# Gate and up of two SwiGLU FFNs: eight block products against seven

## The chip, the cores and the metric

One core of one Trainium2 chip runs the whole kernel. The metric is the device time of one execution in microseconds; a profile of one execution gives each engine's instructions within its span, from the first to the last instruction. TensorE is called PE here, VectorE DVE, ScalarE ACT, GpSimd POOL and SyncE SP; SP issues the DMAs.

## The reference

The kernel computes a two-layer decoder trunk on 512 tokens of 1024 features in float32. Each layer has a token mixer (sparse attention in layer 0, latent attention with an indexer in layer 1), a cross-attention to 256 memory rows, an output projection with a residual, and then a SwiGLU FFN with a residual; a last RMSNorm follows. What matters here is the FFN of each layer, in short:

```python
D_FF = -(-8 * D_MODEL // (3 * 256)) * 256          # 2816
xn = rmsnorm(x, norm_ffn[i])                       # [512, 1024]
h = silu(xn @ ffn_gate[i]) * (xn @ ffn_up[i])      # [512, 2816]
x = x + h @ ffn_down[i]                            # [512, 1024]
```

## The kernel before

**Arithmetic.** Every large product is made of three matmuls. An operand is split into a high part `hi` (the value rounded to the fp32r type) and a low part `lo` (the value minus `hi`); `mm3` (L266) adds hi x hi, hi x lo and lo x hi into one PSUM bank, on L267, L268 and L269. `split` (L213) makes the parts: ACT casts `hi` (L214), DVE subtracts to get `lo` (L215). `split_pool` (L225) does both on POOL, `split_ap` (L229) the cast on ACT and the difference on POOL.

**The FFN.** `ffn` (L592) cuts the 2816 hidden columns into 11 units of 256 and these into four parts, of 3, 3, 3 and 2 units. For a unit, `ffn_gu` (L587) loads 256 columns of gate and of up, 1 MB each, into two tiles `rawb` and splits each into two pieces of 128 columns x 8 k tiles (`whi`, `wlo`, 128x1024 each). For each 128 columns, gate and up are each one PSUM bank of 512 tokens, 8 k tiles x 3 matmuls of 512 columns. In the first unit of a layer the tokens are taken in two halves of 256 columns, so that it can begin when two token tiles have been normed. Then come Silu on ACT (L611), the product with up on DVE (L612) and a split of the result into a hidden tile pair `hh`, `hl`. After the units of a part the down product follows: for each half of the 1024 output columns four PSUM tiles, one for each token tile, over the part's k tiles, in groups of at most four k tiles; DVE adds the finished bank to the residual (L667, in the last part L646).

**Buffers.** `whi` and `wlo` have WBF = 4 buffers each in the FFN, `rawb` 2, the low hidden tiles `hl` 12. The high hidden tiles are held in pairs in the slots of the weight pool of the stage before (`hidden`, L118). PSUM has eight banks in four tags (L42): s 2, t 3, o 2, f 1; `phase` gives each role a string of tags that `bank` goes through in turn. In the FFN (PF, L49) role f, the gate and up banks, goes through o, o, f, t and role s, the down banks, through s, s, t. The tiles `fh`, `fl` (each 128 x 8 x 512) hold the split and transposed input X; `xh` and `xl` hold the concatenated heads until the output projection is done.

**Around it.** The last stage of `out_units` (L547) takes one token tile after another: output projection, residual, `norm_steps` (L174: squares on ACT, scale of the first 512 features on DVE, L207, of the second on POOL, L204 and L205), and `to_T` (L217: transposes on PE, L221, and a split into `fh`, `fl`). `before_ffn` (L982) opens the weight pool of the FFN and loads and splits the first unit ahead of it. In layer 0 `mem_kv1` (L1096), the keys and values of the memory for layer 1, runs after the gate and up of part 0 and before its down product (OTP = 0). In the last part of layer 0 the norm of layer 1 and its first projections (`in_proj`, L998) follow each token tile.

**What sets the order.** The tile framework orders each engine's instructions at compile time, by the order of the program and by when an operand and a buffer come free, so an engine may take a later step ahead of one that still waits. At run time each engine keeps to that order. SP takes the DMAs in its own fixed order; each waits for its slot.

Of the kernel before, what the change touches and what calls it, by code (L numbers as in the profile page):

```python
# [11 lines left out]
OP = mybir.AluOpType  # L12
# [36 lines left out]
PF = ("sst","","","ooft","ooft")  # L49
# [47 lines left out]
def tile_trunk(ctx: ExitStack, tc: tile.TileContext, A, out):  # L97
# [20 lines left out]
    def hidden():  # L118
        WP["n"] = WP.get("n", 0) + 1
        return WP["h"].tile([128, 2, 512], F32R, name=nm("hh"), tag=("raw", "whi", "wlo")[WP["n"] % 3], bufs=2)  # L120


# [10 lines left out]
    # ---------------------------------------------------------------- constants  # L133
# [10 lines left out]
    # ---------------------------------------------------------------- PSUM tiles: one bank each in the mixers  # L144
# [29 lines left out]
    def norm_steps(g, np_, use, by_pool, use_half=None):  # L174
        """(after the first half of the columns of a token tile, after the second half)"""
# [83 lines left out]
    def wsplit(src, by_col, where=None, eng=split):  # L259
        """src [128, a, b] in DRAM -> list of (hi, lo) pieces, cut along b (by 128) or along a"""  # L260
# [10 lines left out]
    def proj_T(xh, xl, nk, W, n, evac, N=512, tag="f", eng=split, where=None):  # L271
        """psum[cols 128, N] for each 128 columns of W [nk*128, n]"""
# [10 lines left out]
    def proj_tok(xh, xl, nk, load, n, evac, step, nt=NT, tag="f"):  # L283
        """psum[tokens 128, n] for each token tile, the weights [nk, 128, n] kept for all of them"""
# [14 lines left out]
    def stack_hl(p, scale, dsts):  # L299
        """p psum [128, N] of two heads -> per head [hi; lo] (even) and [lo; hi] (odd)"""  # L300
# [6 lines left out]
    def dup_hl(p, hi, lo):  # L307
        """p psum [64, ...] -> hi, lo on both halves of the partitions"""
# [4 lines left out]
    # ---------------------------------------------------------------- relative bias rows  # L313
# [34 lines left out]
    # ---------------------------------------------------------------- memory attention  # L348
    def mem_kv(i, xm, rs, wk, kv, slot, f32=False, where=None):
# [14 lines left out]
        proj_T(mt[:, 0], mt[:, 1], KD, W[:, 0:256], 256, ek, N=MEML, eng=ENG[MWK[i][0]], where=where)  # L364
# [9 lines left out]
        proj_tok(mt[:, 0], mt[:, 1], KD, rows(W[:, 256:512], where, ENG[MWK[i][1]]), 256, ev, 4, nt=2)  # L374
# [12 lines left out]
    def pt_piece(work, blocks, bufs, by_pool=False, wide=4):  # L387
        """transposes of [128, 128] blocks -> hi, lo [128, n*128]"""
# [22 lines left out]
    def pt_f32(work, blocks, bufs, wide):  # L411
        """transposes of [128, 128] blocks in float32"""
# [11 lines left out]
    def mem_attend(qm, kv, work, dst, f32=False):  # L424
        """a generator: one step for each pair of query tiles and pair of heads"""
# [161 lines left out]
    def ffn_gu(i, fp, c, eng=split):  # L587
# [4 lines left out]
    def ffn(i, fp, gu0, xh, xl, res, fin, early=None, other=None):  # L592
        Wd = A["ffn_down"][i]
        parts = [(0, 3), (3, 6), (6, 9), (9, 11)]
        for pi, (a, b) in enumerate(parts):
            hh, hl = [], []
            for c in range(a, b):
                gs, us = ffn_gu(i, fp, c) if c else gu0
                hp = hidden()
                for m in range(2):  # L600
                    pp = []
                    for wh, wl in (gs[m], us[m]):
                        p = bank("f")
                        first = c == 0
                        for n0, n1 in ((0, 256), (256, 512)) if first else ((0, 512),):
                            for k in range(KD):
                                mm3(p[:, n0:n1], wh[:, k], wl[:, k], xh[:, k, n0:n1], xl[:, k, n0:n1],
                                    k == 0, k == KD - 1)
                        pp.append(p)
                    sg = fp.tile([128, 512], F32, name=nm("sg"), tag="sg", bufs=2)  # L610
                    act.activation(sg, pp[0], AF.Silu)  # L611
# [721 lines left out]
```

## Time and profile before

| | |
|---|---|
| time of the runs | 1342.33, 1344.34, 1344.53 us (median 1344.34) |
| profiled execution, its span | 1342.6 us |
| PE, DVE, ACT, POOL busy | 1272.7, 724.5, 551.3, 285.6 us |
| matmuls | 6370 |
| mean granted clock | 0.985 of full speed |

The profile gives the profiled execution's span and no other time of its own; the span lies within the times of the runs, 1.7 us under their median. A row of a group reads: line, engine, operation, written tile <- read tiles, shape written <- shape read, count, then busy time in us and mean ns of one, and the idle time of the engine just before them with what ended it. Matmuls are pipelined and their ends are modelled, so that the busy time of several overlaps: their rate is read from their number in a stretch.

### The profile page before, as it was taken

Reading aid. Unit: us, or ns where it says so; the run is one execution under the profiler, and the core shown is the slowest. Engines: PE = TensorE matmul, PEld = TensorE weight load, DVE = VectorE, ACT = ScalarE, POOL = GpSimd, SP = SyncE. Lnnn points to the kernel's source line nnn. Section 1 sums busy time; section 2 is a strip of 40 time slices with the busy share of each in tenths; the row PEclk is TensorE's granted clock in tenths of the full one; section 3 lists DMA queues with packets and bytes.
Section 4 is the critical chain, followed back from the end, with each engine's and each line's share of the span. In section 5 each row is a group of like instructions: output and inputs, shape, how many; then the busy total and the mean of one; then the engine's idle time right before and its main releaser. Section 6 shows DMA issues by size and latency. Waiting matters only on the chain.

```text
span 1342.6 us, 17159 instructions
## 1 busy us (share of the span) xinstructions
PE 1272.7 (95%) x6370; PEld 1041.5 (78%) x6370; DVE 724.5 (54%) x1435; ACT 551.3 (41%) x1146; POOL 285.6 (21%) x442
## 2 busy tenths in 40 slices
PE   5989999999999999999999878999899999999997
PEld 5768889798878888888877655678788888888885
DVE  6475778987334333333445899769633333433325
ACT  6375557775322221221334465556432222222231
POOL 6440445635010000000005165552500000000001
PEclk9999999999999999999999989999899999999998
DMA  7742311223224322322321011324221321321311
GB/s 246 215 139 86 110 41 56 69 74 111 95 94 156 113 76 94 109 75 99 103 94 52 22 61 30 94 77 130 79 94 63 126 94 63 125 94 63 126 63 63
DMA packets 107703, 126.77 MB, mean 94 GB/s; under 512 B 5176, under 2 KB 82008, under 8 KB 107620
## 3 DMA queue, kind: packets, MB, share of 16 engines
q1 hardware_dynamic: 107620, 125.68, 28.8%
q8 instruction: 50, 0.82, 0.3%
q14 instruction: 33, 0.27, 0.1%
HBM read 122.22 MB, written 6.58 MB: 96 GB/s over the span
## 4 chain that ended last, share of the span: by engine, by line
PE 61%; DVE 5%; ACT 2%; POOL 2%; issue 1%; DMA 0%; POOLq 0%; DVEq 0%; ACTq 0%
PE f L267 13%; PE f L268 12%; PE f L269 12%; PE s L268 6%; PE s L269 6%; PE s L267 6%; PE o L532 1%; DVE sco L1131 1%; DVE m L1130 1%; PE t L416 1%; DVE sco L1060 1%; POOL xn L204 1%; PE o L464 0%; DVE sb L511 0%; POOL xn L205 0%
## 5 line engine op out<-in xcount | busy, mean ns | idle before, releaser
L214 ACT CAST whi<-rawb 128x1024 fp32r<-128x1024 f32 (+1 forms) x130 | 135.5, 1048 | 461.4 <-PE f L268 276.7
L267 PE MATMUL f<-fh,whi 128*128 128x512 f32 (+1 forms) x768 | 290.5, 380 | 1.9 <-ACT whi L214 1.2
L268 PE MATMUL f<-fl,whi 128*128 128x512 f32 (+1 forms) x768 | 290.6, 379 | 0.0
L269 PE MATMUL f<-fh,wlo 128*128 128x512 f32 (+1 forms) x768 | 290.2, 379 | 0.3 <-DVE wlo L215 0.3
L215 DVE TENSOR_TENSOR wlo<-rawb,whi 128x1024 fp32r<-128x1024 f32 (+1 forms) x130 | 161.1, 1241 | 220.9 <-ACT whi L214 216.9
L267 PEld LDWEIGHTS f<-fh,whi 128*128 128x128 f32 x768 | 145.8, 191 | 31.9 <-ACT whi L214 1.6
L269 PEld LDWEIGHTS f<-fh,wlo 128*128 128x128 f32 x768 | 145.8, 190 | 30.1 <-DVE wlo L215 0.7
L268 PEld LDWEIGHTS f<-fl,whi 128*128 128x128 f32 x768 | 145.8, 190 | 29.3
L183 POOL TENSOR_SCALAR ss<-ss 128x1 f32<-128x1 f32 x16 | 5.6, 350 | 689.2 <-ACT sq L181 689.2
L612 DVE TENSOR_TENSOR sg<-f,sg 128x512 f32<-128x512 f32 x44 | 30.4, 692 | 177.5 <-PE f L269 176.2
L268 PE MATMUL s<-wlo,hh 128*128 128x512 f32 x288 | 115.0, 399 | 0.0
L267 PE MATMUL s<-whi,hh 128*128 128x512 f32 x288 | 112.3, 394 | 0.0
L269 PE MATMUL s<-whi,hl 128*128 128x512 f32 x288 | 111.6, 390 | 0.0
L521 POOL TENSOR_SCALAR sb<-sb,sm 128x128 f32<-128x128 f32 (+3 forms) x144 | 76.6, 548 | 94.5 <-DVE sm L1218 44.7
L517 ACT ACTIVATE sb<-sb,mx 128x128 f32<-128x128 f32 (+3 forms) x144 | 79.5, 555 | 33.7 <-DVE mx L514 33.0
L511 DVE CUSTOM_DVE_ANT_0 sb<-s,M 128x512 f32<-128x512 f32 (+3 forms) x144 | 66.2, 483 | 13.8 <-PE t L416 4.6
L667 DVE TENSOR_TENSOR res<-s,res 128x512 f32<-128x512 f32 x48 | 32.9, 689 | 60.1 <-PE s L269 60.0
L267 PEld LDWEIGHTS s<-whi,hh 128*128 128x128 f32 x288 | 53.9, 187 | 14.2
L269 PEld LDWEIGHTS s<-whi,hl 128*128 128x128 f32 x288 | 54.1, 188 | 12.8
L268 PEld LDWEIGHTS s<-wlo,hh 128*128 128x128 f32 x288 | 54.0, 188 | 12.0
L215 DVE TENSOR_TENSOR ptl<-t,pth 128x512 fp32r<-128x512 f32 (+1 forms) x98 | 57.6, 603 | 4.7 <-ACT pth L214 3.7
L214 ACT CAST pth<-t 128x512 fp32r<-128x512 f32 (+1 forms) x98 | 48.8, 521 | 22.8 <-PE t L392 19.5
(363 smaller groups left out, 2495.4 us busy)
## 6 DMA issues: line engine op xcount, KB each, us to landing
rawb<-in_ffn_gate_dram SPq DMA_DIRECT2D x22, 1024.0 KB, 5.0
rawb<-in_ffn_up_dram SPq DMA_DIRECT2D x22, 1024.0 KB, 5.5
rawb<-in_ffn_down_dram SPq DMA_DIRECT2D x16, 1024.0 KB, 4.9
M<-relskew SPq DMA_DIRECT2D x36, 256.0 KB, 2.7
raw<-in_w_out_dram SPq DMA_DIRECT2D x16, 512.0 KB, 3.5
raw<-in_nsa_w_in_dram SPq DMA_DIRECT2D x12, 512.0 KB, 4.5
rawb<-in_ffn_down_dram SPq DMA_DIRECT2D x12, 512.0 KB, 3.4
relskew<-relrow SPq DMA_DIRECT2D x1, 3072.0 KB
```

The lines of the kernel that those rows point to most:

```text
L204: pool.tensor_scalar(dst[:, c], src[:, c], r, 0.0, op0=OP.mult, op1=OP.add)
L214: act.copy(hi, src)
L215: dve.tensor_sub(lo, src, f(hi))
L267: pe.matmul(o, ah, bh, start=start, stop=False)
L268: pe.matmul(o, ah, bl, start=False, stop=False)
L269: pe.matmul(o, al, bh, start=False, stop=stop)
L416: pe.transpose(p[:, j * 128:(j + 1) * 128], b, ident)
L511: dve.tensor_tensor_reduce(E[j, br].rearrange("p (k n) -> p k n", n=128), sv[:, :, x, :], Mi.rearrange("p (k n) -> p k n", n=128), 1.0, -3 ...
L517: act.activation(E[j, br], E[j, br], AF.Exp, bias=mx[:, j, br:br + 1], accum_out=sm[:, j, br:br + 1])
L521: pool.tensor_scalar(E[j, br], E[j, br], fc[:, j, br:br + 1], 0.0, op0=OP.mult, op1=OP.add)
L612: dve.tensor_mul(sg, pp[1], sg)
L667: dve.tensor_add(res[t][:, cs], acc[t], res[t][:, cs])
```

## The change

Gate and up are computed by a seven-product scheme on two-by-two blocks. A unit's gate and up weights are each cut into 2 x 2 blocks, A11, A12 (k tiles 0 to 3 and 4 to 7 of the first 128 columns) and A21, A22 (of the second); X is cut into four blocks by k half and token half (B11, B21 for tokens 0 to 255, B12, B22 for 256 to 511). Seven products of a block of weights (for gate and for up at once, 8 k tiles in all) with 256 tokens replace eight. On the X side the sums T1 to T4 are made once for a layer (`x_halves`), on the weight side four sums a unit, on POOL, in place in the raw tile (`gu_unit`). The partial sums are kept in two PSUM banks: four products add into `xb`, three into `z`, and what an output needs on the way is copied out (`c11`, `c12`, `c22`) or added (`tensor_add`).

With it go: a raw tile of 2 MB for a unit (`gu_load`; two buffers); PSUM roles X (tag o, two banks) and Z (tag f, one bank), transposes on tag t; hidden tiles of 128x1024 in eight slots (`hslot`), some of them lent from and to the norm's scratch (`Lent`); the first two products of the first two units taken ahead of the rest of the first unit, in place of the token halves; `mem_kv1` moved to the start of part 1, its memory rows now in a `rawb` slot and its transposes in hidden slots (`Two`); the last part's down weights in the piece slots (`wsplit`).

```diff
-PF = ("sst","","","ooft","ooft")
+PF = ("sst","","","t","t","o","f")
...
+    def hslot(dt=F32R):
+        tag = HS["order"][HS["n"] % len(HS["order"])]
+        HS["n"] += 1
+        where = HS["fp"] if tag == "hx" else WP["h"]
+        return where.tile([128, 1024], dt, name=nm("hh"), tag=tag, bufs=2)
...
-    def phase(s, t, o, f, x):
-        PS.update(s=s, t=t, o=o, f=f, x=x)
+    def phase(s, t, o, f, x, X="", Z=""):
+        PS.update(s=s, t=t, o=o, f=f, x=x, X=X, Z=Z)
...
+    def x_halves(fp):
+
+        fh, fl, th, tl = [big.tile([128, 2 if n == "fl" else 4, 4, 256], F32R, name=nm("X" + n), tag=n)
+                          for n in ("fh", "fl", "xh", "xl")]
+        X = dict(B11=fh[:, 0:2], B21=fh[:, 2:4], B22=fl[:, 0:2], T1=th[:, 0:2], T3=th[:, 2:4], T2=tl[:, 0:2],
+                 T4=tl[:, 2:4])
+        own = []
+
+        def use(t, xn):
+            if not own:
+                own.extend(WP["p"].tile([128, 4, 256], F32, name=nm("xf"), tag=x, bufs=WP["w"]) for x in ("whi", "wlo"))
+            f11, f21 = own
+            q = slice(t % 2 * 128, (t % 2 + 1) * 128)
+            for k0 in (0, 4):
+                p = bank("x")
+                for k in range(4):
+                    pe.transpose(p[:, k * 128:(k + 1) * 128], xn[:, (k0 + k) * 128:(k0 + k + 1) * 128], ident)
+                pv = p.rearrange("p (k q) -> p k q", k=4)
+                if t < 2:
+                    d = X["B21" if k0 else "B11"]
+                    split(pv, d[:, 0, :, q], d[:, 1, :, q])
+                    act.copy((f21 if k0 else f11)[:, :, q], pv)
+                elif k0 == 0:
+                    f12, t1, t3, t2, t4 = [ctile(fp, n).rearrange("p (k q) -> p k q", k=4)
+                                           for n in ("e", "c11", "c12", "c22", "c21")]
+                    dve.tensor_sub(t1, f11[:, :, q], pv)
+                    act.copy(f12, pv)
+                else:
+                    dve.scalar_tensor_tensor(t2, t1, -1.0, pv, op0=OP.mult, op1=OP.subtract)
+                    dve.tensor_sub(t3, pv, f12)
+                    d = X["B22"]
+                    split(pv, d[:, 0, :, q], d[:, 1, :, q])
+                    dve.scalar_tensor_tensor(t4, t2, -1.0, f21[:, :, q], op0=OP.mult, op1=OP.subtract)
+                    for n, x, eng in (("T2", t2, split), ("T1", t1, split_ap), ("T3", t3, split), ("T4", t4, split_ap)):
+                        eng(x, X[n][:, 0, :, q], X[n][:, 1, :, q])
...
+    def gu_load(i, fp, c):
         cs = slice(c * 256, (c + 1) * 256)
-        return [wsplit(A[n][i][:, cs].rearrange("(k p) c -> p k c", p=128), True, fp, eng)
-                for n in ("ffn_gate", "ffn_up")]
-
+        R = fp.tile([128, 2, 8, 2, 128], F32, name=nm("rawb"), tag="rawb", bufs=2)
+        for m, n in enumerate(("ffn_gate", "ffn_up")):
+            dma(R[:, m].rearrange("p k i c -> p k (i c)"), A[n][i][:, cs].rearrange("(k p) c -> p k c", p=128))
+        return R
+
+    def gu_unit(i, fp, c, R, X, hh, hl):
+
+        A11, A12, A21, A22 = R[:, :, 0:4, 0, :], R[:, :, 4:8, 0, :], R[:, :, 0:4, 1, :], R[:, :, 4:8, 1, :]
+        xb = bank("X")
+        st = {}
+
+        def piece(src):
+            hi, lo = [WP["p"].tile([128, 2, 4, 128], F32R, name=nm(x), tag=x, bufs=WP["w"]) for x in ("whi", "wlo")]
+            split(src, hi, lo)
+            return hi, lo
+
+        def prod(o, w, x, first):
+            xh, xl = X[x][:, 0], X[x][:, 1]
+            for m in range(2):
+                oc = o[:, m * 256:(m + 1) * 256]
+                for k in range(4):
+                    a, b = w[0][:, m, k], w[1][:, m, k]
+                    pe.matmul(oc, a, xh[:, k], start=first and m == 0 and k == 0, stop=False,
+                              skip_group_check=True)
+                    pe.matmul(oc, a, xl[:, k], start=False, stop=False, skip_group_check=True)
+                    pe.matmul(oc, b, xh[:, k], start=False, stop=m == 1 and k == 3, skip_group_check=True)
+
+        def hid(m, half, g, u, sign):
+
+            d = ctile(fp, "c21") if m == 1 and half == 0 else None
+            sg, h = (d[:, 0:256], d[:, 256:512]) if d is not None else (g, u)
+            act.activation(sg, g, AF.Silu, scale=sign)
+            if sign > 0:
+                dve.tensor_mul(h, u, sg)
+            else:
+                dve.scalar_tensor_tensor(h, u, -1.0, sg, op0=OP.mult, op1=OP.mult)
+            q = slice(m * 512 + half * 256, m * 512 + half * 256 + 256)
+            split(h, hh[:, q], hl[:, q])
+
+        G, U = slice(0, 256), slice(256, 512)
+        prod(xb, piece(A11), "B11", True)
+        c11 = ctile(fp, "c11")
+        act.copy(c11, xb)
+        yield
+        z = bank("Z")
+        prod(z, piece(A12), "B21", True)
+        dve.tensor_add(c11, z, c11)
+        hid(0, 0, c11[:, G], c11[:, U], 1.0)
+        yield
+        s1 = fp.tile([128, 2, 4, 128], F32, name=nm("S"), tag="S", bufs=1)
+        pool.tensor_add(s1, A21, A22)
+        pool.tensor_add(A21, A11, A21)
+        pool.tensor_add(A11, s1, A11)
+        pool.tensor_add(A12, A11, A12)
+        prod(xb, piece(A11), "T2", False)
+        c12 = ctile(fp, "c12")
+        act.copy(c12, xb)
+        yield
+        z = bank("Z")
+        prod(z, piece(s1), "T1", True)
+        c22 = ctile(fp, "c22")
+        act.copy(c22, z)
+        yield
+        prod(xb, piece(A21), "T3", False)
+        dve.tensor_add(c22, xb, c22)
+        hid(1, 1, c22[:, G], c22[:, U], -1.0)
+        yield
+        prod(z, piece(A12), "B22", False)
+        dve.tensor_add(c12, z, c12)
+        hid(0, 1, c12[:, G], c12[:, U], 1.0)
+        yield
+        prod(xb, piece(A22), "T4", False)
+        hid(1, 0, xb[:, G], xb[:, U], -1.0)
+        yield
...
             for c in range(a, b):
...
+                hs.append((hslot(), hslot()))
+                R = gu_load(i, fp, c) if c else gu0[0]
+                u = gu_unit(i, fp, c, R, X, *hs[-1])
+                if c == 0:
+                    next(u)
+                    next(u)
+                    units.append(u)
+                    continue
+                if c == 1:
+                    next(u)
+                    next(u)
+                    drain(units.pop())
+                drain(u)
...
         np_ = Lent(ng, dict(xn=(fp, "hx", 2), sq=(fp, "S", 1)))
         hslots(fp, ("raw", "whi", "hx", "hx", "wlo", "raw", "whi", "wlo"))
```

## Rows read from the trace of the kernel before

**Rows 1.** The page: span, and busy time of each engine.
```profile
span 1342.6 us, 17159 instructions
...
PE 1272.7 (95%) x6370; PEld 1041.5 (78%) x6370; DVE 724.5 (54%) x1435; ACT 551.3 (41%) x1146; POOL 285.6 (21%) x442
```
**Rows 2.** The page: busy tenths and granted clock in 40 slices of 33.6 us.
```profile
PE   5989999999999999999999878999899999999997
...
PEclk9999999999999999999999989999899999999998
```
**Rows 3.** The page: the chain that ended last, its shares by line.
```profile
PE f L267 13%; PE f L268 12%; PE f L269 12%; PE s L268 6%; PE s L269 6%; PE s L267 6%; PE o L532 1%; DVE sco L1131 1%; DVE m L1130 1%; PE t L416 1%; DVE sco L1060 1%; POOL xn L204 1%; PE o L464 0%; DVE sb L511 0%; POOL xn L205 0%
```
**Rows 4.** Busy time by stretch, all engines: length, busy (count), clock, DMA.
```profile
core 0: us, PE busy (x) PEld busy (x) DVE busy (x) ACT busy (x) POOL busy (x), PEclk, DMA share, GB/s
...
500.00:560.00 60.00, 60.00 (x258) 48.28 (x257) 21.05 (x24) 12.96 (x15) 0.00 (x0) 1.00 0.29 97
```
**Rows 5.** Groups of PE by shape, L268 (L267 and L269 have the same counts).
```profile
L268 PE MATMUL f<-fl,whi 128*128 128x512 f32 x640 | 253.8, 396 | 0.0
...
L268 PE MATMUL s<-wlo,hh 128*128 128x512 f32 x288 | 115.0, 399 | 0.0
...
L268 PE MATMUL f<-fl,whi 128*128 128x256 f32 x128 | 36.8, 292 | 0.0
```
**Rows 6.** Busy time by stretch of what writes or reads tile f alone (PE, PEld, DVE, ACT).
```profile
330.00:342.00 12.00, 11.81 (x100) 11.62 (x99) 0.69 (x1) 0.60 (x1) 1.00 0.34 119
...
500.00:560.00 60.00, 26.75 (x114) 21.26 (x113) 1.38 (x2) 1.19 (x2) 1.00 0.29 97
```
**Rows 7.** Groups of PE's weight loads by shape.
```profile
L268 PEld LDWEIGHTS f<-fl,whi 128*128 128x128 f32 x768 | 145.8, 190 | 29.3
```
**Rows 8.** Groups of ACT by shape.
```profile
L214 ACT CAST whi<-rawb 128x1024 fp32r<-128x1024 f32 x126 | 131.9, 1051 | 461.0 <-PE f L268 276.7 <-PE s L269 136.4 <-DMA rawb<-in_ffn_gate_dram 32.0
...
L419 ACT COPY ptf<-t 128x512 f32<-128x512 f32 x14 | 7.9, 590 | 5.3 <-PE t L416 5.0 <-PE o L532 0.3
...
L214 ACT CAST cat<-ocat 128x256 fp32r<-128x256 f32 x14 | 5.6, 403 | 3.8 <-DVE ocat L383 3.8
...
L1050 ACT ACTIVATE in1c<-s 128x256 f32<-128x256 f32 x8 | 2.9, 381 | 3.8 <-PE s L1045 3.2 <-DVE sco L1060 0.6
```
**Rows 9.** Groups of DVE by shape.
```profile
L215 DVE TENSOR_TENSOR wlo<-rawb,whi 128x1024 fp32r<-128x1024 f32 x126 | 156.9, 1245 | 219.6 <-ACT whi L214 215.6
L569 DVE TENSOR_TENSOR res<-f,res 128x512 f32<-128x512 f32 x64 | 43.6, 685 | 8.6 <-PE f L269 7.9
...
L215 DVE TENSOR_TENSOR cat<-o,cat 128x256 fp32r<-128x256 f32 x10 | 4.2, 417 | 2.4 <-ACT cat L214 2.4
```
**Rows 10.** Groups of POOL by shape.
```profile
L231 POOL TENSOR_TENSOR wlo<-rawb,whi 128x1024 fp32r<-128x1024 f32 x2 | 4.8, 2380 | 60.4 <-ACT whi L230 57.2 <-PE x L221 3.2
...
L1211 POOL TENSOR_TENSOR k2l<-prf,k2h 128x512 fp32r<-128x512 f32 x6 | 7.8, 1297 | 2.8 <-ACT k2h L1210 2.7
```
**Rows 11.** Timeline of DVE and POOL: start, length in us, what.
```profile
324.65 1.60 POOL L205 TENSOR_TENSOR xn<-xn,g 128x512 f32<-128x512 f32 x1
...
325.02 2.31 DVE L215 TENSOR_TENSOR wlo<-rawb,whi 128x1024 fp32r<-128x1024 f32 x1
...
391.72 2.35 POOL L231 TENSOR_TENSOR wlo<-rawb,whi 128x1024 fp32r<-128x1024 f32 x1 [3.21 <-PE x L221]
...
392.77 1.86 DVE L215 TENSOR_TENSOR hl<-sg,hh 128x512 fp32r<-128x512 f32 x1
```
**Rows 12.** Busy time by stretch, columns as in rows 4.
```profile
317.00:330.00 13.00, 11.25 (x76) 10.28 (x77) 11.53 (x12) 8.65 (x16) 10.83 (x12) 0.87 0.63 215
...
385.00:410.00 25.00, 22.66 (x145) 20.55 (x144) 10.97 (x16) 11.37 (x21) 4.76 (x2) 0.93 0.30 106
```
**Rows 13.** Timeline at the two FFN starts: PE, SP's second weight DMA, PE.
```profile
317.51 0.39 PE L267 MATMUL f<-fh,whi 128*128 128x256 f32 x1 [0.74 <-ACT whi L214]
...
951.17 0.37 SPq L263 DMA_DIRECT2D rawb<-in_ffn_up_dram  x1
...
955.40 0.58 PE L267 MATMUL f<-fh,whi 128*128 128x256 f32 x1 [0.73 <-ACT fh L214]
```

More of the change, by code (lines that the diff above doesn't have):

```diff
@@ L116, in weights, with hslots, __init__, __getitem__ @@
         WP.update(es=es, w=wb, r=rb, p=es.enter_context(tc.tile_pool(name=nm("wp"), bufs=1, side="right", reuse_waits="tile")))
-    def hidden():
-        WP["n"] = WP.get("n", 0) + 1
-        return WP["h"].tile([128, 2, 512], F32R, name=nm("hh"), tag=("raw", "whi", "wlo")[WP["n"] % 3], bufs=2)
+    HS = {}
+    def hslots(fp, order):
+        HS.update(fp=fp, order=order, n=0)
+    def hslot(dt=F32R):
[3 more added lines that the diff above has]
+        return where.tile([128, 1024], dt, name=nm("hh"), tag=tag, bufs=2)
+    class Two:
+        def __init__(self, a, b):
+            self.t = a, b
+        def __getitem__(self, at):
+            p, k, n = at
+            if isinstance(k, slice):
+                return self.t[k.start // 4][p, 0:k.stop - k.start, n]
+            return self.t[k // 4][p, k % 4, n]
+    class Lent:
+        def __init__(self, own, lent):
+            self.own, self.lent = own, lent
+        def tile(self, shape, dt, name=None, tag=None, bufs=1):
+            if tag in self.lent:
+                where, tag, bufs = self.lent[tag]
+                return where.tile(shape, dt, name=name, tag=tag, bufs=bufs)
+            return self.own.tile(shape, dt, name=name, tag=tag, bufs=bufs)
     def nm(s):
@@ L585, in out_units, with ctile @@
                 yield
-    def ffn_gu(i, fp, c, eng=split):
-        cs = slice(c * 256, (c + 1) * 256)
-        return [wsplit(A[n][i][:, cs].rearrange("(k p) c -> p k c", p=128), True, fp, eng)
-                for n in ("ffn_gate", "ffn_up")]
-    def ffn(i, fp, gu0, xh, xl, res, fin, early=None, other=None):
+    def ctile(fp, tag):
+        return fp.tile([128, 512], F32, name=nm(tag), tag=tag, bufs=1)
+    def x_halves(fp):
[31 more added lines that the diff above has]
+                        eng(x, X[n][:, 0, :, q], X[n][:, 1, :, q])
+        return X, use
@@ L593, in ffn @@
+    def ffn(i, fp, gu0, X, res, fin, early=None, other=None):
         Wd = A["ffn_down"][i]
@@ L595, in ffn @@
         for pi, (a, b) in enumerate(parts):
-            hh, hl = [], []
+            hs = []
+            units = []
+            if other and pi == 1:
+                other()
             for c in range(a, b):
[L598 to L611, printed above, removed]
-                    dve.tensor_mul(sg, pp[1], sg)
-                    h1 = hp[:, m]
-                    h2 = fp.tile([128, 512], F32R, name=nm("hl"), tag="hl", bufs=12)
-                    split(sg, h1, h2)
-                    hh.append(h1)
-                    hl.append(h2)
+                hs.append((hslot(), hslot()))
[11 more added lines that the diff above has]
+                drain(u)
+            hh, hl = [[x[j][:, m * 512:(m + 1) * 512] for x in hs for m in range(2)] for j in range(2)]
             last = pi == len(parts) - 1
-            if other and pi == OTP:
-                other()
             nk = 2 * (b - a)
@@ L626, in ffn @@
                     src = Wd[a * 256:b * 256, half * 512:(half + 1) * 512]
-                    rv = wraw(0, fp).rearrange("p (k c) -> p k c", c=512)
-                    dma(rv, src.rearrange("(k p) c -> p k c", p=128))
-                    ws = []
-                    for k in range(nk):
-                        if k % 2 == 0:
-                            hp = hidden()
-                        hl_ = [hp[:, k % 2], fp.tile([128, 512], F32R, name=nm("hl"), tag="hl", bufs=12)]
-                        split(rv[:, k, :], *hl_)
-                        ws.append(hl_)
-                    both.append(ws)
+                    both.append([(wh[:, j, :], wl[:, j, :])
+                                 for wh, wl in wsplit(src.rearrange("(k p) c -> p k c", p=128), False, fp)
+                                 for j in range(wh.shape[1])])
                 pre, after = fin()
@@ L714, in tile_trunk @@
                 slot = big.tile([128, 4096], F32R, name="mt0", tag="fh")
-                mem_kv(0, xm, rs, sp, kv0, slot)
+                slot = slot.rearrange("p (a k q) -> p a k q", a=2, k=KD)
+                mem_kv(0, xm, rs, sp, kv0, [slot[:, a] for a in range(2)])
                 g = gain(A["norm_mix"][0], sp)
@@ L983, in before_ffn @@
             weights(WBF, over=True)
[L984 to L987 removed]
+            gu0.append(gu_load(0, fp, 0))
+        X, to_X = x_halves(fp)
         phase(*PL0)
         drain(out_units(STL0, A["w_out"][0], cat, None, res, split,
[L990 removed]
+                        *norm_steps(gain(A["norm_ffn"][0], np_), np_, to_X, NSP), before_ffn))
         phase(*PF)
```

38 lines of the change are left out of this document (18 added, 20 removed).

## The prediction

> **What bounds the kernel now.** I read the page from the top. PE is busy for 1272.7 of 1342.6 us, DVE for 724.5 [rows 1]. By slices PE stands at nine tenths or more nearly everywhere, most evenly in the two FFNs (from 317.5 and from 955.4 us on, slices 10 to 21 and 29 to 40), at a granted clock of nine tenths and over [rows 2, 13]. The chain that ended last is PE work on the three lines of mm3, 37% of the span into the FFN's tile f [rows 3]. A 60 us stretch inside the first FFN shows the balance there: PE 60.00, DVE 21.05, ACT 12.96, POOL 0 [rows 4]. So a gate and up unit costs what PE needs for its columns, and all other engines have room.
>
> The groups by shape say how many matmuls that is [rows 5]: 640 of 512 columns and 128 of 256 on each of three lines. They make 20 units of 96 x 512 columns, and two units (the first of each layer) of 192 x 256. Busy times of matmuls overlap, so I take the price from one tile's share of a stretch: 26.75 us for 114 of 512 columns, 0.235 us each; 11.81 us for 100 of 256 columns, 0.118 us each [rows 6]. Half the columns cost half the time, although each matmul loads its weights and one load is 0.190 us long [rows 7]: the loads are hidden behind one another and behind the matmuls, and a hundred matmuls in a row show it.
>
> **The change, part by part.**
>
> *PE.* A unit becomes 7 products x 2 (gate, up) x 4 k tiles x 3 = 168 matmuls of 256 columns: 168 x 0.118 = 19.8 us. Before it was 96 x 0.235 = 22.6 us, in the first unit of a layer 192 x 0.118 = 22.7 us. That removes 20 x 2.8 + 2 x 2.9 = 61 us, all of it from the path; I take 60. The down products keep their count.
>
> *ACT and DVE in a unit.* Seven pieces in place of four. ACT: 7 x 1.05, three copies of a bank 0.59 each, four Silu of 256 columns 0.38, four casts 0.40 [rows 8]: 7.4 + 1.8 + 1.5 + 1.6 = 12.3 us. DVE: 7 x 1.245, three bank additions of 0.685, four products and four differences of 256 columns at 0.417 [rows 9]: 8.7 + 2.1 + 3.3 = 14.1 us. Both lie under 19.8 us of PE, so as work they cost nothing; the pieces are made four ahead (WBF = 4), which is 4 x 2.83 = 11.3 us of cover.
>
> *POOL in a unit.* Four additions of 128x1024 with both inputs in SBUF; the nearest row is the difference of the same size, 2.38 us [rows 10]: 9.5 us, again under 19.8.
>
> *DVE against POOL.* These two are not independent. A DVE difference of 128x1024 from SBUF, 1.245 us as a rule, took 2.31 us when it began at 325.02, while a POOL product ran from 324.65 to 326.25; one of 128x512 took 1.86 us beside a POOL operation of 391.72 to 394.07 [rows 11]: each ended about its own length after POOL was done. So operations with two SBUF inputs take turns. In a unit those are 9.5 us of POOL and, on DVE, 8.7 + 7 x 0.417 = 11.6 us (the additions and the last product read PSUM): 21.1 us against 19.8 of PE. A part falls behind by 1.3 us a unit, 3.9 us in three, and the pieces are 11.3 us ahead; the down products that follow (6 x 4 x 2 x 3 x 0.235 = 33.8 us, no POOL work) let it catch up. As a bound on throughput I therefore take nothing.
> The Trainium skill's page "SBUF — State Buffer", section "Who interferes with whom", states this as a rule: a DVE instruction with two SBUF inputs and a GpSimd instruction that reads SBUF exclude each other for the whole instruction. The four rows agree with it; by that rule alone, with no work done ahead, a unit would be 21.1 us long, which is the first rival below.
>
> *Waits for the two accumulators.* A bank is read out between two products into it, and one product, 2.83 us, lies between. Three read-outs a unit are ACT copies (0.59 us behind at most one cast of 1.05: in time). Three are DVE additions. One of those can find DVE held by POOL and then busy with a piece: 2.38 + 1.245 + 0.685 = 4.3 us, 1.5 us too late for PE. Bounds: 0, and 3 x 1.5 = 4.5 us a unit. Behind a late addition wait, on DVE, the hidden product and the next piece, and on PE the next product into that bank. POOL is at work for half of a unit, and its last two additions come only after the splits whose source they overwrite, so a read-out rarely meets the whole queue: I take the lower part, 0.7 us a unit, 22 x 0.7 = 15 us.
>
> *Start of each FFN.* The work on X grows. For token tiles 2 and 3 DVE has seven operations of about 0.7 us, 4.9 us in place of 2 x 0.685, ACT six of 0.59, POOL two of 1.30 [rows 10]. PE has three products that need only tiles 0 and 1 (3 x 2.83 = 8.5 us); the fourth waits until c11, first the scratch of token tile 3, is free. Before, the first matmuls of layer 0 began at 317.51, and POOL finished the last norm at 326.25 [rows 11, 13]; the stretch ran at 0.87 of the clock with PE idle for 1.75 us [rows 12]. From 326.3: transposes 0.9, DVE and splits to T1 some 4.9 + 1.3, copy and addition 1.3: the fourth product at about 335, and the third unit-0 operand not before POOL's s1 (its slot is lent to the norm's squares, and POOL is in the norms until then), 326.3 + 3 x 2.38 + 2.3 = 336. PE's three products end at about 331. So 4 to 5 us are lost where there was no stall; 0 to 10 as bounds. Behind that wait stands all of PE's later work. Layer 1 is alike: the second of its raw weights is issued at 951.17, and PE starts at 955.40 [rows 13]; the second unit's 2 MB must now follow at once. I take 5 us each, 10 us.
>
> *Memory keys and values of layer 1.* Moved from before to behind the down products of part 0, into slots that those products free last. PE was idle for 25 - 22.66 = 2.3 us there, at a clock of 0.93 [rows 12]: 4 us with the clock. Now four scalings of 0.7, transposes and four splits, some 6 us in a chain, come when no product is left over, for the raw tiles of the next unit queue on SP behind the memory rows and the four memory weights, in the same two slots. POOL's two differences of 2.38 us move with it, ahead of the next unit's additions, which need the raw tiles anyway; the three stores to DRAM are read in layer 1 only. So 6 + 2 - 4 = 4 us are lost (0 to 12).
>
> *End of layer 0.* The last down weights now take all four piece slots, so the first projection's pieces are split after the last token tile: 2 us (0 to 6). SP's DMAs keep their number and bytes; a unit's 2 MB have 19.8 us.
>
> **Sum.** -60 + 15 + 10 + 4 + 2 = -29 us. From the profiled span of 1342.6 us this is 1313.6; the median of the runs is 1344.34, 1.7 us above that span, so I predict 1315 us.
>
> **The rivals.**
> *The shared turn sets the pace.* If the four pieces ahead don't hold, a unit takes 21.1 us: gain 22 x (22.6 - 21.1) = 33, less 16 for starts and ends: 1344 - 17 = 1327 us. For it: 21.1 is over 19.8. Against: the parts are short and the down products carry no POOL work. Chance 0.2.
> *PE waits for late read-outs (slower than before).* The order on DVE is fixed, a blocked DVE delays the addition that frees the bank, and the two accumulators (Z has one buffer, tag f) have no other place to go. At 1.5 us for each of three additions: 22 x 4.5 = 99 us against 60 - 16 = 44 of gain, 1344 + 55 = 1399 us. It decides from 44 / 22 = 2.0 us of PE waits a unit, 0.29 us a product, on. For it: DVE goes from 35% busy to 14.1 of 19.8 us, with another 9.5 in which it can be held. Against: POOL's operations fall mostly where no addition is due. Chance 0.15.
> *No gain from fewer columns.* If a matmul of 256 columns cost its weight load, 0.190 us, a unit would be 31.9 us and the kernel 1344 + 22 x 9.3 = 1549 us. The hundred matmuls at 0.118 us speak against it: 0.02.
>
> **How the numbers follow.** Forecast 0.63, rivals 0.2, 0.15, 0.02. With all lower bounds of the losses the gain is 60 less a few, 1290; with the upper bounds of starts and ends (20 + 12 + 6) and 0.7 us a unit it is 1337; the lock rival lies within, and its upper side reaches no change. I give 1293 to 1345; the tail outside is mostly the slower rival. What a measurement here can tell is about 0.2%, 2.7 us. Faster: nearly all of the forecast and most of the first rival, 0.80; same: the rest of it, 0.05; slower 0.15.
>
> **What would show it.** Right: gate and up matmuls of 256 columns, 3696 in all, about 0.118 us apart; a middle unit of 20 to 21 us; POOL about 9.5 us a unit; DVE differences of 1.2 us with some of 2 to 3; PE idle near the start of each FFN. Wrong: PE waits for DVE additions or ACT copies of a bank above 2 us a unit, or a PE that waits for pieces in the third unit of each part.

## The result and the profile after

The changed kernel takes 1357.11 us (median of 4 runs, 1354.00 to 1359.32) against 1343.93 us (1342.33 to 1344.53) for the kernel before, run beside it: a ratio of 1.0098, interval 1.008 to 1.0116. It is slower by 1%; 1315 us were forecast, and the time lies above the range. The profiled execution has a span of 1354.2 us.

Lines of the changed kernel that the text below uses: L243 and L244 are the cast and the difference of a split, L681, L683 and L684 the three matmuls of a product, L701 the copy of the first product's bank to c11, L705 the addition of the second product's bank to it, L709 to L712 the four sums of weight blocks (s, A21', A11', A12'), L715 the copy of the third product's bank, L690 and L692 or L694 Silu and the hidden product, L635 the transposes of X, L234 and L236 the norm's scaling on POOL and on DVE. Units are counted from 0 in a layer, and a layer's four parts too.

The page of the changed kernel (engines, slices of 33.9 us, chain), to be read against [rows 1 to 3]:

```profile
PE 1231.6 (91%) x7762; PEld 1086.1 (80%) x7762; DVE 991.8 (73%) x1667; ACT 673.3 (50%) x1382; POOL 537.3 (40%) x538
...
PE   5989999997699899999999878899759999999997
...
DVE  6475779987883686685677799759777497497485
...
POOL 7440445638420540440515155543762161251241
PEclk9999999998799999999999889999879999999999
...
PE 56%; DVE 20%; POOL 7%; issue 6%; DMA 5%; ACT 5%; SPq 1%; POOLq 0%; DVEq 0%; ACTq 0%
DVE wlo L244 7%; PE s L297 5%; PE s L296 5%; PE s L298 5%; PE f L296 4%; PE X L681 4%; PE X L683 3%; PE X L684 3%; PE f L297 3%; PE f L298 3%; PE Z L681 3%; PE Z L684 3%; PE Z L683 3%; PE t L420 2%; DVE hh L244 2%
```

PE is busy for 41 us less, DVE for 267 us more, and the first line of the chain is now DVE's difference of a piece. The clock dips where the two FFNs start (slices 10 to 11 and 29 to 30).

Two stretches by engine, as [rows 4, 12]: part 0 of layer 0 and part 1 of layer 1, of the changed kernel:

```profile
320.00:409.00 89.00, 70.11 (x521) 68.22 (x520) 72.75 (x71) 44.00 (x70) 42.73 (x22) 0.84 0.17 58
...
1087.40:1153.80 66.40, 62.90 (x509) 62.04 (x509) 56.60 (x54) 34.29 (x54) 23.98 (x10) 0.97 0.22 72
```

Three units on PE should have taken 3 x 19.8 = 59.4 us. Part 1 of layer 1 takes 66.4, with PE idle for 3.5 us, and part 0 of layer 0 takes 89.0. What PE waits for (us in total, times, longest):

```profile
PE Z L681 <- DVE c L705: 16.9, 6, 3.3
PE x L635 <- POOL xn L234: 13.4, 4, 6.8
...
PE X L681 <- ACT c L701: 8.8, 4, 6.0
...
PE X L683 <- DVE Xxl L244: 6.2, 2, 3.2
```

The six waits for L705 stand one in each part of three units. One of them, in the middle of layer 1's FFN, on the timeline (start, length in us, what):

```profile
1112.51 2.40 POOL L709 TENSOR_TENSOR S<-rawb 128x1024 f32<-128x1024 f32 x1 [2.97 <-DVE wlo L244]
1114.99 2.44 POOL L710 TENSOR_TENSOR rawb<-rawb 128x1024 f32<-128x1024 f32 x1
...
1112.35 0.41 DVE L694 SCALAR_TENSOR_TENSOR c<-X,c 128x256 f32<-128x256 f32 x1
1112.68 2.51 DVE L244 TENSOR_TENSOR hh<-c,hh 128x256 fp32r<-128x256 f32 x1
1115.12 3.40 DVE L244 TENSOR_TENSOR wlo<-rawb,whi 128x1024 fp32r<-128x1024 f32 x1
1118.44 0.41 DVE L244 TENSOR_TENSOR hh<-c,hh 128x256 fp32r<-128x256 f32 x1
1118.77 0.68 DVE L705 TENSOR_TENSOR c<-Z,c 128x512 f32<-128x512 f32 x1
...
1119.50 0.58 PE L681 MATMUL Z<-Xxh,whi 128*128 128x256 f32 x1 [2.81 <-DVE c L705]
```

Two of POOL's sums stand one right behind the other, 0.08 us apart. A DVE difference of 256 columns, 0.41 us alone, lasts until the first sum is over; the piece's difference behind it, 1.2 us alone, until 1.1 us after the second. From the start of the first of the two, DVE needs 6.1 us to reach L705, and PE stands still for 2.8 us before 1119.50. Then it runs slowly. The busy time in the wait and in the 3.4 us after it (the clock is the third column from the right):

```profile
1116.50:1119.30 2.80, 0.20 (x2) 0.00 (x0) 2.80 (x3) 0.00 (x0) 0.93 (x1) 0.99 0.00 0
1119.30:1122.70 3.40, 3.20 (x15) 3.20 (x16) 3.14 (x5) 2.15 (x4) 0.00 (x0) 0.50 0.02 5
```

At a granted clock of 0.50 (1.2 GHz) 3.4 us do the work of 1.7. So the wait costs 2.8 + 1.7 = 4.5 of the 5.5 us that the stretch has above the 60.9 us it takes without such waits (experiment 1). Behind each of the other five waits, of 2.4 to 3.3 us, the granted clock falls to one half likewise.

### The profile page after: what moved, and what is told of

Its sections match the earlier page's. It is cut to its first block, busy times and chain, and to the rows that moved or that the text cites. A ratio compares the mean times of both kernels' runs of the same rounds, so it can differ in the third digit from the quotient of the medians.

```text
span 1354.2 us, 20724 instructions
## 1 busy us (share of the span) xinstructions
PE 1231.6 (91%) x7762; PEld 1086.1 (80%) x7762; DVE 991.8 (73%) x1667; ACT 673.3 (50%) x1382; POOL 537.3 (40%) x538
## 4 chain that ended last, share of the span: by engine, by line
PE 56%; DVE 20%; POOL 7%; issue 6%; DMA 5%; ACT 5%; SPq 1%; POOLq 0%; DVEq 0%; ACTq 0%
DVE wlo L244 7%; PE s L297 5%; PE s L296 5%; PE s L298 5%; PE f L296 4%; PE X L681 4%; PE X L683 3%; PE X L684 3%; PE f L297 3%; PE f L298 3%; PE Z L681 3%; PE Z L684 3%; PE Z L683 3%; PE t L420 2%; DVE hh L244 2%
## 5 line engine op out<-in xcount | busy, mean ns | idle before, releaser
L244 DVE TENSOR_TENSOR wlo<-rawb,whi 128x1024 fp32r<-128x1024 f32 (+1 forms) x182 | 294.5, 1622 | 123.5 <-ACT whi L243 123.1
L243 ACT CAST whi<-rawb 128x1024 fp32r<-128x1024 f32 (+1 forms) x182 | 189.8, 1047 | 247.4 <-PE s L298 101.4
L709 POOL TENSOR_TENSOR S<-rawb 128x1024 f32<-128x1024 f32 x22 | 58.8, 2671 | 279.2 <-DMA rawb<-in_ffn_up_dram 249.3
L298 PE MATMUL s<-whi,hh 128*128 128x512 f32 x352 | 137.4, 392 | 0.0
L296 PE MATMUL s<-whi,hh 128*128 128x512 f32 x352 | 133.7, 391 | 0.0
L549 POOL TENSOR_SCALAR sb<-sb,sm 128x128 f32<-128x128 f32 (+3 forms) x144 | 77.3, 554 | 93.9 <-DVE sm L1350 44.0
L681 PE MATMUL X<-Xxl,whi 128*128 128x256 f32 x352 | 101.8, 289 | 9.3 <-ACT c L701 8.8
L683 PE MATMUL X<-Xxl,whi 128*128 128x256 f32 x352 | 101.5, 288 | 6.2 <-DVE Xxl L244 6.2
L684 PE MATMUL X<-Xxl,wlo 128*128 128x256 f32 x352 | 101.2, 288 | 1.9 <-DVE wlo L244 1.9
L545 ACT ACTIVATE sb<-sb,mx 128x128 f32<-128x128 f32 (+3 forms) x144 | 79.5, 555 | 33.2 <-DVE mx L542 32.5
L711 POOL TENSOR_TENSOR rawb<-S,rawb 128x1024 f32<-128x1024 f32 x22 | 57.2, 2602 | 67.4 <-DVE wlo L244 66.8
L243 ACT CAST hh<-c 128x256 fp32r<-128x256 f32 x88 | 35.8, 407 | 88.0 <-DVE c L694 44.4
L681 PEld LDWEIGHTS X<-Xxl,whi 128*128 128x128 f32 x352 | 68.9, 196 | 10.7 <-ACT c L701 10.0
L298 PEld LDWEIGHTS s<-whi,hh 128*128 128x128 f32 x352 | 66.1, 188 | 14.1
L296 PEld LDWEIGHTS s<-whi,hh 128*128 128x128 f32 x352 | 65.5, 188 | 13.7
L683 PEld LDWEIGHTS X<-Xxl,whi 128*128 128x128 f32 x352 | 68.8, 195 | 6.8 <-DVE Xxl L244 6.8
L244 DVE TENSOR_TENSOR hh<-c,hh 128x256 fp32r<-128x256 f32 x88 | 68.5, 779 | 4.1 <-ACT hh L243 3.8
L684 PEld LDWEIGHTS X<-Xxl,wlo 128*128 128x128 f32 x352 | 69.0, 196 | 2.2 <-DVE wlo L244 2.2
L681 PE MATMUL Z<-Xxh,whi 128*128 128x256 f32 x176 | 54.4, 309 | 16.9 <-DVE c L705 16.9
```

The source lines that it names most:

```text
L243: act.copy(hi, src)
L244: dve.tensor_sub(lo, src, f(hi))
L296: pe.matmul(o, ah, bh, start=start, stop=False)
L298: pe.matmul(o, al, bh, start=False, stop=stop)
L545: act.activation(E[j, br], E[j, br], AF.Exp, bias=mx[:, j, br:br + 1], accum_out=sm[:, j, br:br + 1])
L549: pool.tensor_scalar(E[j, br], E[j, br], fc[:, j, br:br + 1], 0.0, op0=OP.mult, op1=OP.add)
```

## The experiments

The parts of all kernels in one table, in us from the first to the last gate and up matmul of a part in the trace (part 0 of layers 0 / 1, part 1 of layers 0 / 1, part 2 of layer 1), the time, and its ratio to runs of the kernel before beside it. In part 2, and in part 1 of the kernel before, some matmuls of the part run ahead among the down products; the 4 us of down products in between are left out. Experiments 1 and 5 leave out work that the result needs; they are there to price it.

| kernel | part 0 | part 1 | part 2 | us | ratio, interval |
|---|---|---|---|---|---|
| before | 73.3 / 73.7 | 67.8 / 67.8 | 67.8 | 1343.93 | 1 |
| changed | 89.2 / 90.0 | 72.1 / 66.4 | 66.3 | 1357.11 | 1.0098, 1.008 to 1.0116 |
| 1: no sums | 74.1 / 73.6 | 61.4 / 60.9 | 60.9 | 1296.44 | 0.965, 0.9616 to 0.9683 |
| 2: sums of unit 0 late | 89.3 / 88.6 | 71.4 / 66.7 | 66.5 | 1358.05 | 1.0108, 1.0088 to 1.0128 |
| 3: sums on DVE | 79.6 / 82.1 | 61.7 / 60.9 | 60.9 | 1312.18 | 0.9765, 0.9749 to 0.978 |
| 4: Z in two banks | 83.5 / 87.6 | 74.1 / 69.6 | 69.9 | 1381.09 | 1.0274, 1.023 to 1.0319 |
| 5: no sums, light X | 67.2 / 66.7 | 61.2 / 60.9 | 60.9 | 1282.72 | 0.9549, 0.9535 to 0.9563 |
| 6: units 0, 1 on DVE | 80.0 / 82.9 | 71.9 / 66.5 | 66.3 | 1342.59 | 0.9992, 0.9972 to 1.0011 |
| 7: as 3, T1 apart | 76.9 / 77.4 | 61.5 / 61.2 | 60.9 | 1304.75 | 0.971, 0.9696 to 0.9725 |
| 8: as 7, last sum on POOL | 77.3 / 80.1 | 64.6 / 61.9 | 61.6 | 1314.88 | 0.9785, 0.9753 to 0.9818 |
| 9: as 7, last two on POOL | 78.9 / 80.7 | 64.6 / 61.3 | 61.3 | 1317.16 | 0.9807, 0.9774 to 0.9839 |
| 10: as 7, first two on POOL | 80.2 / 86.3 | 71.6 / 63.2 | 63.2 | 1334.89 | 0.9929, 0.9908 to 0.995 |
| 11: as 7, first on POOL | 79.5 / 78.4 | 63.2 / 61.0 | 61.0 | 1312.38 | 0.9766, 0.9752 to 0.9781 |

**1. No sums.**

```diff
-        s1 = fp.tile([128, 2, 4, 128], F32, name=nm("S"), tag="S", bufs=1)
-        pool.tensor_add(s1, A21, A22)
...
-        pool.tensor_add(A12, A11, A12)
+        s1 = A21
```

> Leaves the four weight sums on POOL out (88 operations in all) and takes the raw blocks in their place, so the hidden values are other ones; everything else stays. Theory A (POOL's sums cost by turns with DVE and by their place in POOL's queue): the unit in the middle falls from 22.0 to 20.0 us, the first part of each layer (gate and up from its first product to its end, 89 to 90 us) to about 70, and the time to about 1305 us. Theory B (single banks, late read-outs whatever POOL does): the unit stays at 21.5 us and over, 1345 us or more. Theory C (the added work on X sets the start): the units recover, the first parts stay at 80 us and over, about 1335 us.

Part 1 of layer 1, busy time by engine:

```profile
1041.80:1102.40 60.60, 60.60 (x509) 60.43 (x509) 40.58 (x53) 33.18 (x51) 0.00 (x0) 1.00 0.24 78
```

PE has no gap and full clock. DVE does the same 53 or 54 instructions in 40.6 us that take 56.6 beside ten sums: 16 us of its busy time are turns, and in the whole kernel 991.8 - 867.6 = 124 us. The sums cost 1357.1 - 1296.4 = 61 us, about as much as the cheaper products give; 15 and 16 of them lie in the two parts 0.

**2. Unit 0's sums behind the norms on POOL**, by the place of a scratch tile.

```diff
-                                           for n in ("e", "c11", "c12", "c22", "c21")]
+                                           for n in ("S" if t == 3 else "e", "c11", "c12", "c22", "c21")]
```

> The scratch of the last token tile lies in the slot of POOL's first sum, so that the sums of the first unit come behind the norms in POOL's queue; nothing else changes. Theory A: the second half of the last norm comes some 10 us earlier in each layer, the first part shrinks by 10 to 15 us, the time falls by 20 to 30 us, to about 1332 us; units in the middle stay at 22.0 us. Theory C (X work and the reuse of its scratch set the start): no change beyond 5 us.

The order did change: POOL is done with the last norm 6.8 us after the first product of layer 0's FFN begins, against 18.2 us in the changed kernel. But part 0 stays at 89 us. PE's waits there have other names (from 315 to 412 us):

```profile
PE X L681 <- ACT whi L243: 6.9, 1, 6.9
PE Z L681 <- DVE c L705: 5.6, 1, 5.6
PE X L681 <- ACT c L715: 3.5, 1, 3.5
```

So it is not the place of the first unit's sums in POOL's queue alone: with the norm out of their way, products wait for a piece and for read-outs instead.

**3. All sums on DVE.**

```diff
-        pool.tensor_add(s1, A21, A22)
+        dve.tensor_add(s1, A21, A22)
```

and so for the other three.

> The four sums on DVE in place of POOL. Theory A: the turns are gone; DVE has 14.1 + 4 x 1.23 = 19.0 us of work a unit, just under PE's 19.9; a unit in the middle at 20.5 to 21 us and the first parts at 75 to 80 us, about 1325 us. A rival (DVE is simply full, and it makes no difference which engine holds the port): units at 22 us or more, 1350 us or more.

PE is without a gap in part 1 of layer 1 again, as without sums, and the kernel is faster than both the changed kernel and the one before. A sum takes DVE 1.22 to 1.29 us of its own on the mean; on POOL it takes 2.3 to 3.4 us and costs DVE 16 / 10 = 1.6 us of waiting in the stretch of experiment 1, in lumps.

**4. Z in two banks**, so that L705 has one product more of time.

```diff
-PF = ("sst","","","t","t","o","f")
+PF = ("sst","","","t","t","o","ft")
```

> The second accumulator Z goes through two tags (f, t) in turn, so that a Z product need not wait for the read-out of the one before. Theory B: the waits for L705 (16.9 us of PE in six places, and the half clock behind them) go, 20 us or more are gained, about 1335 us. Theory A: DVE is the engine that paces, the same time is lost one or two products later on another read-out or on a piece; within 6 us of 1357.

The wait for L705 is gone, another is there, and the kernel is slower still; neither expectation had that. PE's largest wait, and the timeline of the end of one:

```profile
PE X L681 <- ACT c L715: 34.8, 13, 4.5
```

```profile
1319.36 3.20 POOL L710 TENSOR_TENSOR rawb<-rawb 128x1024 f32<-128x1024 f32 x1
1320.29 2.56 DVE L692 TENSOR_TENSOR c<-c 128x256 f32<-128x256 f32 x1
1322.88 0.41 ACT L243 CAST hh<-c 128x256 fp32r<-128x256 f32 x1 [4.81 <-DVE c L692]
1323.19 1.04 ACT L243 CAST whi<-rawb 128x1024 fp32r<-128x1024 f32 x1
...
1324.14 0.58 ACT L715 COPY c<-X 128x512 f32<-128x512 f32 x1
```

The third product had ended at 1317.8, but ACT keeps its order: it stands idle for 4.8 us until its cast of the hidden half gets a product (L692) that POOL holds up on DVE, and behind the cast stand a piece and the copy L715 that frees X. A second bank does not help: the delay sits on DVE and comes out at another read-out. Z now shares tag t with the transposes; whether that adds to the 24 us above the changed kernel was not tried.

**5. No sums, and a light X.**

```diff
-        X = dict(B11=fh[:, 0:2], B21=fh[:, 2:4], B22=fl[:, 0:2], T1=th[:, 0:2], T3=th[:, 2:4], T2=tl[:, 0:2],
-                 T4=tl[:, 2:4])
+        b22 = fl[:, 0:2]
+        X = dict(B11=fh[:, 0:2], B21=fh[:, 2:4], B22=b22, T1=b22, T3=b22, T2=b22, T4=b22)
...
```

The lines of `x_halves` that make and split the combinations are left out, and the four sums as in experiment 1.

> Leaves out, beside the four sums of each unit as in the first experiment, the combinations of the activations and their splits: the products with T1 to T4 read B22 in their place, and the products, matmuls and other work are the same. Without the sums the gate and up of part 0 took 74.1 and 73.6 us against 59.6 us of matmuls. Theory (the combinations on DVE, ACT and POOL are the most of what is lost there, some 9 us per FFN above the 5.6 us of the kernel before): part 0 near 65 us, 1278 us in all. Rival (what is lost there is the order of units 0 and 1 and their pieces of weights, which stays): 74 us and 1296 us.

Part 0 is 6.9 us shorter than in experiment 1 in both layers, 13.7 us in all: that is the price of the combinations of X. The 6 us that stay above 60.9 were there before too (73.3 and 73.7 against 67.8). This kernel stands 62 us under the kernel before. From the first to the last gate and up matmul of a layer it takes 343.5 and 325.1 us for 371.6 and 354.3: 57 us are the cheaper products' (X being lighter here than it was before, at most that). Another 8 us in all are gained behind the last gate and up product of the two layers, and the first product of layer 0 begins 6 us later.

**6. Units 0 and 1 on DVE, the rest on POOL.**

```diff
-        pool.tensor_add(s1, A21, A22)
...
+        sm = dve if c < 2 else pool
+        sm.tensor_add(s1, A21, A22)
...
```

and so for the other three.

> The sums on DVE for units 0 and 1 alone, on POOL for the nine that follow. Theory (the loss at the two starts and the loss in the middle are two separate prices of the same sums): part 0 about 80 to 82 us in place of 89 to 90, parts 1 to 3 as in the changed kernel (66 us, 42 us), 1339 us in all. Rival (unit 2's sums, which POOL has now earlier, hold up DVE in the start as before, or DVE's own sums there cost what POOL's did): part 0 near 89 us, 1357 us; and if parts 1 to 3 came out at 61 us, the middle would have suffered from the start's delay and not from POOL: 1312 us.

1342.6 us for the 1339 of the theory: two separate prices. The start falls to what it is in experiment 3, parts 1 and 2 stay as in the changed kernel. Of the 45 us between that kernel and experiment 3, 14.5 are the start's and 30 the middle's.

**7. T1 of token tile 3 out of c11's slot**, all sums on DVE.

```diff
-                                           for n in ("e", "c11", "c12", "c22", "c21")]
+                                           for n in ("e", "S" if t == 3 else "c11", "c12", "c22", "c21")]
```

> As the third experiment (all sums on DVE), and T1 of token tile 3 in the slot of the weights' sum in place of c11's, so that unit 0's first read-out (c11, L701) need not wait until POOL has split T1. In the third experiment PE waited 4.9 us for that read-out and part 0 took 79.6 and 82.1 us. Theory (the shared slot holds up the read-out, and with it PE): up to 4 us less per FFN, 1304 to 1308 us. Rival (DVE has no gap from the first combination to unit 0's last product, so its work sets the time wherever the scratch lies): 1312 us.

Both parts 0 are shorter (by 2.7 and 4.7 us), and this is the fastest version that leaves nothing out, 3% under the kernel before. Part 0 of layer 0 and part 1 of layer 1:

```profile
323.70:400.60 76.90, 68.49 (x523) 67.27 (x522) 66.02 (x82) 43.85 (x71) 11.85 (x10) 0.89 0.21 69
1048.50:1109.60 61.10, 61.10 (x510) 60.73 (x509) 49.94 (x62) 33.38 (x51) 0.00 (x0) 1.00 0.23 78
```

In the middle PE is the bound again, as [rows 4] had it. At the start DVE is busy for 66 of 76.9 us and PE's wait for L701 (4.9 us in experiment 3) is gone; what remains is a piece of A11', 6.9 us late in its place (5.4 us in layer 1).

**8 to 11. One or two sums on POOL**, the others on DVE as in experiment 7; the edit is shown against that one. 8:

```diff
-        dve.tensor_add(A12, A11, A12)
+        pool.tensor_add(A12, A11, A12)
```

> As the seventh experiment (sums on DVE, T1 apart), and the last of the four sums (A12', L712) on POOL. Theory (PE waits in the middle because two sums stand one behind the other on POOL, so that DVE loses two turns ahead of a late read-out; one sum alone costs DVE one turn, which unit and pieces in reserve take up): parts 1 to 3 stay at 61 and 40.5 us, 1303 to 1308 us in all. Rival (each sum on POOL has the same price, a quarter of the 52 us between the changed kernel and the seventh experiment): 13 us more, 1318 us, part 2 near 62.3 us.

9: L711 and L712 on POOL.

> As before it, with the last two sums (A11' and A12', L711 and L712) on POOL; A12' needs A11', so they can follow each other. Theory (two in a row cost two turns): the step from one to two sums on POOL is far larger than the step from none to one; parts of three units at 63 us or more, 1320 us or more in all, if the two do run in a row; if the trace shows a gap between them (A11' has to wait for DVE's last read of the old A11), they count as single ones and the time stays under 1310 us. Rival (same price for each): 1331 us, part 2 near 63.6 us.

10: L709 and L710 on POOL.

> As the seventh experiment (sums on DVE, T1 apart), with the first two sums (s and A21', L709 and L710) on POOL, which stand back to back in the trace of the changed kernel; the last two stay on DVE. In the ninth experiment the last two on POOL, 1.2 us apart, cost 12 us. Theory (it is the two sums in a row that make DVE miss its time): most of the 52 us between the changed kernel and the seventh experiment comes back, 1335 us or more, parts of three units at 64 us or more. Rival (any two sums on POOL have the price of the last two): 1317 us, parts near 61.5 us.

11: L709 alone on POOL.

> As before it, with the first sum (s, L709) alone on POOL and A21' on DVE. Theory (one sum alone costs one turn, wherever in the unit): as the eighth experiment, 1312 to 1317 us, parts of three units at 61 to 62 us. Rival (the place of the first sum, ahead of the late read-out of L705, is what costs, not that a second follows it): as the experiment before it, 1335 us or more.

One sum costs 8 us (experiment 11) or 10 us (8), more than the 3 that the theory of experiment 8 allowed, of which part 2 of layer 1 has 0.1 and 0.7; most of the rest is in part 0 and in part 1 of layer 0, and some 2 us lie between the FFNs, which the edit does not touch. The last two cost 12 us. By the intervals, some 4 us either way in experiments 8 and 9, these three prices can't be told apart. The last two are not back to back, POOL's timeline in experiment 9:

```profile
1075.14 2.41 POOL L711 TENSOR_TENSOR rawb<-S,rawb 128x1024 f32<-128x1024 f32 x1 [12.44 <-DVE wlo L244]
1078.78 2.47 POOL L712 TENSOR_TENSOR rawb<-rawb 128x1024 f32<-128x1024 f32 x1 [1.23 <-DVE wlo L244]
```

The first two cost 30 us, well apart from the others, and in experiment 10 the timeline of POOL and DVE repeats the changed kernel's:

```profile
1099.88 2.40 POOL L709 TENSOR_TENSOR S<-rawb 128x1024 f32<-128x1024 f32 x1 [12.05 <-DVE wlo L244]
1102.36 2.46 POOL L710 TENSOR_TENSOR rawb<-rawb 128x1024 f32<-128x1024 f32 x1
...
1100.05 2.51 DVE L244 TENSOR_TENSOR hh<-c,hh 128x256 fp32r<-128x256 f32 x1
1102.49 3.41 DVE L244 TENSOR_TENSOR wlo<-rawb,whi 128x1024 fp32r<-128x1024 f32 x1
1105.82 0.41 DVE L244 TENSOR_TENSOR hh<-c,hh 128x256 fp32r<-128x256 f32 x1
1106.16 0.68 DVE L705 TENSOR_TENSOR c<-Z,c 128x512 f32<-128x512 f32 x1
```

PE's waits for L705 follow it (experiments 9, 10 and 11):

```profile
PE Z L681 <- DVE c L705: 4.7, 8, 1.1
...
PE Z L681 <- DVE c L705: 8.3, 5, 2.0
...
PE Z L681 <- DVE c L705: 0.9, 3, 0.4
```

Part 2 of layer 1 tells the same apart from the starts: 60.9 without POOL, 61.0 with the first sum, 61.3 with the last two, 63.2 with the first two. So there is no fixed price per sum: two sums that DVE can pass between cost well under half of two that follow each other (12 and 30 us; 0.4 and 2.3 in part 2). One rival is left: L710 alone was not tried, so that its place, and not its following L709, could have a part in the 30 us; the timeline, with DVE held by one and then by the other, speaks for the pair. That the theory's own figures are not met everywhere (63.2 for "64 us or more", 12 us for the pair with a gap where under 5.3 was expected) leaves some price for a single sum at the starts. With all four, part 2 takes 66.3, above 63.2 + 0.4. The traces show why: the wait there is 2.8 us long for 2.0 in experiment 10, and the granted clock, which in experiment 10 stays at 1.00 behind three of its four waits of 2.0 us, falls to a half behind each wait of the changed kernel, 1.7 us more.

## Why the prediction was wrong, by its steps

- *PE*, -60 us: right. Experiment 5 finds at most 57 us between the first and the last product of a layer, and a part of three units takes 60.9 us at full clock, some matmuls of the down product included.
- *ACT and DVE in a unit*: right as work. DVE's 14.1 us a unit are 40.6 / 3 = 13.5 in experiment 1, additions to the residual included.
- *DVE against POOL*: the mechanism was right, the conclusion was not. "As a bound on throughput I therefore take nothing" holds to the letter: DVE is busy for 56.6 of 66.4 us. But the turns come as a delay at a place. The Trainium skill's page "SBUF — State Buffer", section "Who interferes with whom", which that step names, gives the exclusion of whole instructions, and the timelines agree (2.51 and 3.40 us for 0.41 and 1.2).
- *Waits for the two accumulators*, +15 us: **this is the step that failed.** It let an addition meet one sum, "2.38 + 1.245 + 0.685", and argued that "a read-out rarely meets the whole queue" because the last two sums come late. The first two come together, and in one unit of each part of three L705 stands behind both. Experiments 9 to 11 show it. The six waits come to 16.9 us, near the 15 by luck: the forecast spread 0.7 us over every unit, and it left out the half clock behind each of the six, 1.7 us. It also left out all else that the sums hold up: the two parts 0 alone lose 15 and 16 us by them (experiment 1), only a part of it in this wait. There PE is idle for 18.9 us of 89.0 at a clock of 0.84, against 6.2 of 74.1 at 0.90 without sums. In all 61 us stood for 15, or 2.8 us for 0.7 a unit; some 27 of them are the six waits with their slow stretches. That the ACT copies are "in time" nearly held in the middle (PE waited 0.8 us for L715 in all), but only as long as Z had one bank: in experiment 4 they come up to 4.5 us late behind a cast that waits for DVE.
- *POOL in a unit*, 9.5 us: four sums of 2.5 to 2.9 us on the mean, 10.7 us; close, and beside the point.
- *Start of each FFN*, 5 us each: 6.9 for the work on X, within its bounds. It put POOL's first sum behind the norms; in the changed kernel that sum begins at 317.84, among them, and the last norm leaves POOL at 338.16. Experiment 2 shows that this order alone is not what the start loses by. It counted no turns. Nor does a run tell the turns there from the mere length of a sum on POOL (2.4 us for 1.2 on DVE), which a piece of A11' has to await.
- *Memory keys and values*, 4 us: PE's stretch without gate, up or down work lasted 17.5 us before and 17.8 after. Part 1 of layer 0, behind it, is 5.7 us longer than that of layer 1, but only with sums on POOL; with none there it is 0.3 to 0.8. Why the two go together was not tried.
- *End of layer 0*, 2 us: a gain and no loss. From the last gate and up matmul of layer 0 to the first of layer 1 it is 266.3 us before and 260.9 after, and from the last of layer 1 to the end of the span 32.9 and 28.2: 10 us in all for which the forecast has no term. Before, PE waited there 1.5 and 1.9 us for the low part of the last hidden tile (L215), and now it does not; what the rest is was not followed up.

From the first to the last gate and up matmul the changed kernel takes 383.9 us for 371.6 in layer 0 and 361.2 for 354.3 in layer 1: 19.2 us more, which experiments 5 and 1 make up as -57.3 (cheaper products), +13.9 (work on X) and +62.6 (sums). With 10.1 us gained behind these stretches and a first product 2.5 us later that is +11.6, as the profiled spans have it (1354.2 for 1342.6). Of the rivals, the slower one came true in its sign, by luck in part: the sums cost 2.8 us a unit, above its point of decision of 2.0, but PE's waits for read-outs, of which it spoke, are 16.9 + 8.8 + 0.8 us or 1.2 a unit. It also blamed the accumulators, and a second bank made things worse. The shared turn as what sets the pace fell: DVE, its waiting included, fills 56.6 of 66.4 us and not all of them.

## What to carry to other kernels

When work is put on an idle engine that shares something with a busy one, don't compare totals: look which of its operations follow each other without a gap, what the busy engine does next behind the blocked operation, and who waits for that. Ask whether the busy engine could do it itself: here 22 x 4 sums of 1.2 to 1.3 us on DVE, which had room, cost less than the same sums on POOL. And price a wait of TensorE together with the granted clock after it: six waits of 2.4 to 3.3 us were each followed by a half clock, of four waits of 2.0 us only one.

## What the runs showed of the hardware

A DVE operation of 0.41 us took 2.51 and its successor 3.40 beside two POOL sums, so DVE got a turn only where one sum ended. The 2.8 us wait was followed by 3.4 us at a granted clock of 0.50. POOL's sum of one size took 2.40 us in some places and 3.3 in others: the sum of 3.32 us that began at 1093.72 in the changed kernel ended 2.3 us after a DVE piece of 1093.56 to 1094.77, so POOL waits for DVE as well.
